# One layer of a hyena and attention backbone: the mixing part's weight remainders and sums moved from GpSimd to VectorE

## The chip, the cores and the metric

The kernel runs on one core of a Trainium2 chip, in float32. The metric is the device time of one execution in microseconds (us), as the median of several runs. TensorE does the matrix products (PE in the profile, PEld its weight loads), VectorE (DVE) and ScalarE (ACT) the elementwise work, GpSimd (POOL) a small share of it, and SyncE (SP) issues the weight transfers.

## The reference

The reference is one layer over 256 latent tokens and 256 context tokens of width 2048. Cut to what matters:

```python
x   = half_ffn(x, ...)                # SwiGLU FFN of width 5632, for latent and context tokens
ctx = half_ffn(ctx, ...)
h, hc = modulate(rms_norm(x)), modulate(rms_norm(ctx))
q, k, v, hy = split_proj(h @ w_in)    # queries, keys, values, and three hyena inputs x0, x1, v
kc, vc = kv_heads(hc @ w_in[:, Q_END:V_END])
attn = block_attention(rope(q), [kc ; rope(k)], [vc ; v])
x0, x1, v = short_conv(hy)            # width 3, centred
v = v * x1
hyo = (long_conv(v) + hy_bias * v) * x0      # convolution through a real FFT of length 512
x = x + gate * (concat(rms_norm(attn), rms_norm(hyo)) @ w_out)
return half_ffn(x, ...)               # second FFN, latent tokens alone
```

## The kernel before, in words

Everything is kept transposed, channels on the 128 partitions and tokens in the free dimension. The full 256 latent and 256 context tokens stand side by side in one 512-column product in the first FFN; the rest of the layer is for latent tokens, with the context only in keys and values.

**A float32 product in pieces.** A float32 operand is cut into a rounded part (`hi`, type fp32r) and a remainder (`lo`), and a product is two or three fp32r products. So each weight tile that arrives (`raw`, 128x1024) needs a cast on ScalarE (`whi`, L192) and a subtraction (`wlo`, L194), before TensorE can use it. The function `weight` does this; its argument `eng` says which engine subtracts, VectorE where none is given:

```python
        S.copy(hi, raw)
        ...
            (eng or V).tensor_sub(lo, raw, hi.bitcast(F32))
```

Activations are cut in the same way (`split` with L176 and L177, `split_to` with L181 and L182; L253 and L254 for the normed inputs). `whi` and `wlo` have three buffers each, `raw` has four.

**The stages of the mixing part, by the time of the profile.** Up to 1533 us the first FFN, of which the last part of the down projection is done twice, first for the context (until 1533) and then for the latent tokens (until about 1556), with the residual sum at L622. While the latent part runs, a hook makes the context's norm: squares on ScalarE (L234), their sums over the eight channel pairs at L241, a product with ones (L245) that adds over partitions, and L215 to L220 for the inverse root. After it come the scaled inputs, one L251, L253 and L254 for each of 16 channel tiles. The projection to keys and values (L653 to L655, `pa`) is done for the context first and then for the latent tokens, with eight weight tiles each, `kp` 0 to 7; the latent norm's steps are put between the context's products by a list in the code, `KV_PLAN`. Then follow the hyena projection (until about 1705), the long convolution (until about 1757; per half and frequency block four products L788 to L791, a difference L796 and a sum L797, and two splits, before the inverse products), and the attention (until about 1850).

**The filler.** The gate `x0` is projected in four column pairs `cp` of four weight tiles `kq` each (`proj_pair`, L208 to L211, 16 matmuls a weight tile, 64 a column pair). It is a generator, of which the attention takes a step where TensorE would wait, and what is left comes at the end of the attention. A column pair's two products lie in two `pa` buffers (there are four for all uses), which come free when L731, the first step of the short convolution (L730 to L734, then L819 multiplies the gate in), has read them. After the attention its group norm (`group_out`: L234, L241, L245, L215 to L220, and then 8 L883 with splits at L181 and L182) gives the first inputs of the output projection `w_o`; the hyena group's norm comes next to its first tiles. The residual's norm (L241, L245) and the second FFN close the layer, from about 1990 on.

**What sets the order.** The code's order is a start only: the framework's scheduler reorders the instructions of each engine by its own costs, and each engine then works off its row in order. So a change of engine moves other instructions as well. The weight transfers are in one queue on SyncE, in the same order before and after.

**The lines on GpSimd before.** `wlo` of every second tile of the last down projection (both parts) and of every second tile of the key and value projection; all 16 `wlo` of the gate; the additions L241 of all norms after the first; L796 and L797; and the `wlo` of every second tile of the second FFN's down projection.

Of the kernel before, what the change touches and what calls it, by code (L numbers as in the profile page):

```python
# [18 lines left out]
P = 128  # L19
# [5 lines left out]
GRP = 4  # L25
# [22 lines left out]
def hybrid_layer_kernel(ctx: ExitStack, tc: tile.TileContext, a):  # L48
    nc = tc.nc
    V, S, G, PE = nc.vector, nc.scalar, nc.gpsimd, nc.tensor  # L50
# [134 lines left out]
    def weight(src, shape, eng=None, behind=None):  # L185
        raw = T(wp, shape, "raw", bufs=4)
        load = nc.sync.dma_start(raw, src)
        if done[0]:
            last_load[0] = load
        hi = T(wp, shape, "whi", F32R, 3)  # L190
        lo = T(wp, shape, "wlo", F32R, 3)
        S.copy(hi, raw)  # L192
        if behind is None:
            (eng or V).tensor_sub(lo, raw, hi.bitcast(F32))  # L194
        else:
            with tc.issue_after(behind.ins):
                V.tensor_sub(lo, raw, hi.bitcast(F32))
        return hi, lo
# [27 lines left out]
    def rstd_steps(pairs, n, y):  # L226

        ps = PB((P, L))
        todo_, acc = [], None
        for q, t in enumerate(pairs):  # L230
            last = q == len(pairs) - 1
            sq = (tmp if last or acc is not None else tmp2)((P, 2, L))
            for part in ((0, 1) if last else (slice(0, 2),)):
                S.activation(sq[:, part, :], t[:, part, :], AF.Square)  # L234
            if last:
                todo_.append(sq)
            elif acc is None:
                acc = sq
                todo_.append(acc)
            else:  # L240
                G.tensor_add(acc, acc, sq)  # L241
        yield
        for q, t in enumerate(todo_):
            for j in range(2):
                PE.matmul(ps, ones, t[:, j, :], start=q == 0 and j == 0, stop=q == len(todo_) - 1 and j == 1)  # L245
        rstd_from(ps, n, (P, L), tmp2, y)
# [22 lines left out]
    class Ffn:  # L269
# [44 lines left out]
        def down(self, g, parts=None, last=None):  # L314

            whole = parts is None
            for dq in range(KT // 2):
                self.hook()
                whi, wlo = weight(self.wdown[g, dq], (P, GRP, 2, P), G if dq % 2 and (not whole or self.np == 1) else None)
                for i2 in range(2):  # L320
                    d = dq * 2 + i2
                    ps = PB((P, 2, L) if whole else (P, L))
                    for jj in range(GRP):
                        act = self.acts[g * GRP + jj]
                        if not whole:
                            act = [t[:, parts, :] for t in act]
                        self.mm(ps, (whi[:, jj, i2, :], wlo[:, jj, i2, :]), act, jj == 0, jj == GRP - 1)
                    if self.np == 1:
                        for half in range(2):
                            V.scalar_tensor_tensor(xd(0, d), ps[:, half, :], mod[0][8][:, d : d + 1], xd(0, d),  # L330
                                                   op0=ALU.mult, op1=ALU.add)
                        if last:
                            last(d)
                        continue
                    for i in range(2) if whole else (parts,):
                        src = ps[:, i, :] if whole else ps
                        if last:
                            last(i, d, src)
                        elif self.gated:
                            V.scalar_tensor_tensor(xd(i, d), src, mod[i][self.cm + 2][:, d : d + 1], xd(i, d),  # L340
                                                   op0=ALU.mult, op1=ALU.add)
                        elif g == 0:
                            S.copy(xd(i, d), src)
                        else:
                            V.tensor_add(xd(i, d), src, xd(i, d))
# [142 lines left out]
    for i in range(2):  # L488
        for q, t in enumerate(xs[i]):
            sq = U((P, 2, L))  # L490
# [18 lines left out]
    for i in range(2):  # L509
        ps = PB((P, L))  # L510
# [32 lines left out]
    with tc.issue_after(copied.ins):  # L543
        w = {j: weight(f1.wup[j, 0], (P, 4, 2, P), behind=lo_last) for j in range(WAVE)}
# [90 lines left out]

    def proj_cols(w, ttiles, share=False, hook=lambda: None):
        ps = []
        for _ in proj_steps(w, ttiles, ps, share):  # L640
            hook()
        return ps

    def proj_steps(w, ttiles, ps, share=False):
        ps += [PA() for _ in ttiles]
        for kp in range(8):
            yield
            whi, wlo = weight(w[kp], (P, 2, 512), G if share and kp % 2 else None)
            for k2 in range(2):
                k = kp * 2 + k2  # L650
                for p_, t in zip(ps, ttiles):
                    hh, hl = ((lat, cont)[t // 2][k][:, s, (t % 2) * P : (t % 2 + 1) * P] for s in range(2))
                    PE.matmul(p_, hh, whi[:, k2, :], start=k == 0, stop=False)  # L653
                    PE.matmul(p_, hh, wlo[:, k2, :], start=False, stop=False)  # L654
                    PE.matmul(p_, hl, whi[:, k2, :], start=False, stop=k == KT - 1)  # L655
# [43 lines left out]
    krot = []  # L699
    also = mix_input(0, lat)  # L700
    plan = iter(KV_PLAN)
    pkv = proj_cols(a["w_kv"], [2, 3], True, lambda: [next((more, also)[s], None) for s in next(plan)])
    for _ in also:
        pass
    pkv += proj_cols(a["w_kv"], [0, 1], True)
    for i in range(4):
        n_ = head_norm(pkv[i], 2)
        if i < 2:
# [26 lines left out]
                               op0=ALU.mult, op1=ALU.add)  # L735
        return y

    def proj_pair(w, out, share=False):
        pa, pb = PA((P, 2, L)), PA((P, 2, L))
        out += [pa, pb]  # L740
        for kq in range(4):
            whi, wlo = weight(w[kq], (P, 4, 2, P), G if share else None)
            for k4 in range(4):
                k = kq * 4 + k4
                for half, ps in ((0, pa), (1, pb)):
                    mm2(ps, (whi[:, k4, half, :], wlo[:, k4, half, :]), lat[k], k == 0, k == KT - 1)
            if kq < 3:
                yield
# [21 lines left out]
    for half in range(2):  # L770
        hs = slice(half * 512, half * 512 + 512)
        vt = []
        for t in range(2):
            pt = PB((P, 4, P))
            for i in range(4):
                ct = half * 4 + i
                PE.transpose(pt[:, i, :], vT[ct // 2][:, ct % 2, t * P : (t + 1) * P], ident)
            vt.append(split(pt.rearrange("p a b -> p (a b)"), (P, 512)))
        yre, yim = [], []
        for f in range(2):  # L780
            pr_, pi_ = PB(), PB()
            for ps, mat in ((pr_, fwd[0]), (pi_, fwd[1])):
                for t in range(2):
                    mm3(ps, [m[:, t, f * P : (f + 1) * P] for m in mat], vt[t], t == 0, t == 1)
            kr, ki = kspec[f][:, hs], kspec[2 + f][:, hs]
            a1, a2 = U((P, 512)), U((P, 512))
            b1, b2 = U((P, 512)), U((P, 512))
            V.tensor_mul(a1, pr_, kr)  # L788
            V.tensor_mul(a2, pi_, ki)
            V.tensor_mul(b1, pr_, ki)  # L790
            V.tensor_mul(b2, pi_, kr)  # L791
            if f == 0:
                V.tensor_copy(b2[0:1, :], a2[0:1, :])
                V.memset(a2[0:1, :], 0.0)
                V.memset(b1[0:1, :], 0.0)
            G.tensor_sub(a1, a1, a2)  # L796
            G.tensor_add(b1, b1, b2)  # L797
            yre.append(split(a1, (P, 512)))
            yim.append(split(b1, (P, 512)))
            for _ in range(QSTEP[2 * half + f]):  # L800
                next(query, None)
        for i in range(4):
            ct = half * 4 + i
            ps = PB((P, L))
            sl = slice(i * P, (i + 1) * P)
            for n, (y_, mat) in enumerate(((yre, inv[0]), (yim, inv[1]))):
                for f in range(2):
                    mm3(ps, [m[:, sl] for m in y_[f]], [m[:, f, :] for m in mat], n + f == 0, n + f == 2)
            V.scalar_tensor_tensor(hyT[ct // 2][:, ct % 2, :], vT[ct // 2][:, ct % 2, :], hyb[:, ct : ct + 1], ps,
                                   op0=ALU.mult, op1=ALU.add)  # L810


    def gate_steps():
        for cp in range(CT // 2):
            p0 = []
            yield from proj_pair(a["w_x0"][cp], p0, True)
            for i in range(2):
                y_ = conv(p0[i], 2 * cp + i)
                V.tensor_mul(hyT[cp][:, i, :], hyT[cp][:, i, :], y_)  # L819
            yield  # L820
# [235 lines left out]
```

## Time and profile before

| What | Value |
|---|---|
| Median of 3 runs | 2743.27 us (2742.76 to 2743.49) |
| Profiled execution | 2740.93 us |
| Its span | 2739.1 us, TensorE clock 0.993 on average |
| TensorE busy | 2680.5 us, 98% |
| VectorE busy | 1866.1 us, 68% |
| GpSimd busy | 235.5 us, 9%, in 113 instructions |
| GpSimd busy from 1480 to 1990 us | 127 us: 32 L194, 22 L241, 4 L796, 4 L797 |
| GpSimd busy after 1990 us | 107.8 us: 44 L194 |

The profiled execution is 2.34 us below the median, and 1.83 us of it lie outside its span. A busy TensorE means only that products follow each other; when it has been idle, the profile's clock column shows whether they run at the full clock. An instruction's duration includes time in which it is held by something that isn't a semaphore, so that the same shape can show two durations; a mean over a line hides this.

### The profile page before, as it was taken

The page shows a single profiled execution, that of the slowest core. Times are in us where ns is not written, and L with a number is a line of the kernel's source. Part 1 is how long each engine was busy: PE and PEld are TensorE (multiplying, and loading weights), DVE is VectorE, ACT ScalarE, POOL GpSimd, SP SyncE. Part 2 cuts the span into 40 slices and gives each one's busy share as a digit, 9 for nine tenths or more (in the row PEclk, how much of TensorE's full clock was granted, in tenths as well). Part 3 has the DMA queues.
Part 4 walks back from the last instruction along what each step waited for, and adds up shares of the span by engine and source line. Part 5 has one row for each costly group of instructions (what it writes and reads, how often), then busy time and mean ns, then how long its engine had stood idle before and what let it go on. Part 6 is the DMA issues. An engine that isn't in the chain of part 4 may idle for free. (4 is left out here: it accounts for less than half of the span.)

```text
span 2739.1 us, 35313 instructions
## 1 busy us (share of the span) xinstructions
PE 2680.5 (98%) x13552; PEld 2232.1 (81%) x13552; DVE 1866.1 (68%) x3044; ACT 962.5 (35%) x1307; POOL 235.5 (9%) x113
## 2 busy tenths in 40 slices
PE   8999999999999999999999999988999999999999
PEld 5678888888888888888888878777788888888888
DVE  6589899976686666434342897878666666666666
ACT  4343222222222222222222555355454444444443
POOL 0000000000000000000000620232111111111111
PEclk9999999999999999999999999999999999999999
DMA  9776666666686666432332455224555555555555
GB/s 381 286 267 213 228 215 219 210 225 210 233 296 224 211 219 216 150 100 96 97 100 93 145 179 185 94 92 140 169 169 185 185 185 186 185 186 187 186 186 170
DMA packets 144352, 513.49 MB, mean 187 GB/s; under 512 B 17175, under 2 KB 21432, under 8 KB 139832
## 3 DMA queue, kind: packets, MB, share of 16 engines
q1 hardware_dynamic: 142456, 508.50, 55.2%
q10 hardware_dynamic: 1728, 2.74, 0.3%
q8 instruction: 107, 1.75, 0.3%
q14 instruction: 61, 0.50, 0.1%
HBM read 506.98 MB, written 4.19 MB: 187 GB/s over the span
## 5 line engine op out<-in xcount | busy, mean ns | idle before, releaser
L192 ACT CAST whi<-raw 128x1024 fp32r<-128x1024 f32 x648 | 680.6, 1051 | 1301.6 <-PE pa L202 489.3
L194 DVE TENSOR_TENSOR wlo<-raw,whi 128x1024 fp32r<-128x1024 f32 x569 | 700.9, 1233 | 490.8 <-ACT whi L192 482.9
L209 PE MATMUL pa<-u,whi 128*128 128x512 f32 x2016 | 715.0, 401 | 10.5 <-DVE u L254 5.9
L201 PE MATMUL pa<-u,whi 128*128 128x512 f32 x1376 | 537.1, 391 | 2.7 <-ACT u L529 2.7
L203 PE MATMUL pa<-u,wlo 128*128 128x512 f32 x1376 | 535.7, 390 | 1.7 <-DVE wlo L194 1.7
L202 PE MATMUL pa<-u,whi 128*128 128x512 f32 x1376 | 536.6, 390 | 0.7 <-DVE u L531 0.7
L211 PE MATMUL pa<-u,wlo 128*128 128x256 f32 x1890 | 533.2, 282 | 2.9 <-POOL wlo L194 1.9
L209 PEld LDWEIGHTS pa<-u,whi 128*128 128x128 f32 x2016 | 377.8, 189 | 98.3 <-issue 6.3
L194 POOL TENSOR_TENSOR wlo<-raw,whi 128x1024 fp32r<-128x1024 f32 x76 | 189.7, 2496 | 2276.3 <-ACT whi L192 2266.0
L211 PEld LDWEIGHTS pa<-u,wlo 128*128 128x128 f32 x1890 | 359.6, 190 | 7.5 <-POOL wlo L194 2.3
L201 PEld LDWEIGHTS pa<-u,whi 128*128 128x128 f32 x1376 | 258.2, 188 | 60.2 <-ACT u L529 4.0
L203 PEld LDWEIGHTS pa<-u,wlo 128*128 128x128 f32 x1376 | 258.1, 188 | 57.6 <-DVE wlo L194 3.1
L202 PEld LDWEIGHTS pa<-u,whi 128*128 128x128 f32 x1376 | 258.6, 188 | 55.3 <-DVE u L531 1.6
L201 PE MATMUL pb<-u,whi 128*128 128x512 f32 (+1 forms) x800 | 299.8, 375 | 2.4 <-DVE u L622 2.4
L203 PE MATMUL pb<-u,wlo 128*128 128x512 f32 (+1 forms) x800 | 298.8, 374 | 2.5 <-DVE wlo L194 2.5
L202 PE MATMUL pb<-u,whi 128*128 128x512 f32 (+1 forms) x800 | 298.7, 374 | 0.0
L209 PE MATMUL pb<-u,whi 128*128 128x512 f32 x736 | 250.3, 399 | 2.2 <-DVE u L330 2.2
L130 DVE CUSTOM_DVE_ANT_0 adas<-adaw,crow,bada 128x1024 bf16<-128x1024 f32 x160 | 205.0, 1281 | 22.1 <-DMA adaw<-in_w_adaT_dram 20.0
L130 DVE CUSTOM_DVE_ANT_0 adas<-adaw,crow,mod 128x1024 bf16<-128x1024 f32 x160 | 205.1, 1282 | 9.8 <-DMA adaw<-in_w_adaT_dram 6.9
L201 PEld LDWEIGHTS pb<-u,whi 128*128 128x128 f32 x800 | 152.0, 190 | 33.7 <-issue 5.0
L203 PEld LDWEIGHTS pb<-u,wlo 128*128 128x128 f32 x800 | 152.1, 190 | 29.0 <-DVE wlo L194 2.7
L202 PEld LDWEIGHTS pb<-u,whi 128*128 128x128 f32 x800 | 151.9, 190 | 26.0
(202 smaller groups left out, 2314.6 us busy)
## 6 DMA issues: line engine op xcount, KB each, us to landing
raw<-in_w_up_dram SPq DMA_DIRECT2D x352, 512.0 KB, 3.6
adaw<-in_w_adaT_dram SPq DMA_DIRECT2D x223, 512.0 KB, 4.9
raw<-in_w_dn_dram SPq DMA_DIRECT2D x184, 512.0 KB, 3.5
wrow<-in_w_ada_dram SPq DMA_DIRECT2D x32, 1024.0 KB, 7.9
raw<-in_w_hy_dram SPq DMA_DIRECT2D x32, 512.0 KB, 3.6
raw<-in_w_o_dram SPq DMA_DIRECT2D x32, 512.0 KB, 3.5
raw<-in_w_kv_dram SPq DMA_DIRECT2D x16, 512.0 KB, 4.1
raw<-in_w_q_dram SPq DMA_DIRECT2D x16, 512.0 KB, 3.5
```

The source lines that it names most:

```text
L130: V.tensor_tensor_reduce(out=sc, in0=t, in1=crow[i][:, b * (D // 2) : (b + 1) * (D // 2)], scale=1.0, scalar=mcol if b else bada[:, n : n ...
L192: S.copy(hi, raw)
L194: (eng or V).tensor_sub(lo, raw, hi.bitcast(F32))
L201: PE.matmul(ps, w[0], xx[0], start=start, stop=False)
L202: PE.matmul(ps, w[0], xx[1], start=False, stop=False)
L203: return PE.matmul(ps, w[1], xx[0], start=False, stop=stop)
L209: PE.matmul(ps, w[0], x, start=start, stop=stop)
L211: PE.matmul(ps[:, 0, :], w[1], x[:, 0, :], start=False, stop=False)
```

## The change

GpSimd keeps only the 44 `wlo` of the second FFN. The 32 other `wlo` subtractions, the 22 additions of squares (L241) and the eight sums of the long convolution (L796, L797) go to VectorE. The same operations are done on the same tiles; 62 instructions change engine.

```diff
@@ rstd_steps
-                G.tensor_add(acc, acc, sq)
+                V.tensor_add(acc, acc, sq)
@@ Ffn.down
-                whi, wlo = weight(self.wdown[g, dq], (P, GRP, 2, P), G if dq % 2 and (not whole or self.np == 1) else None)
+                whi, wlo = weight(self.wdown[g, dq], (P, GRP, 2, P), G if dq % 2 and self.np == 1 else None)
@@ proj_steps (keys and values)
-            whi, wlo = weight(w[kp], (P, 2, 512), G if share and kp % 2 else None)
+            whi, wlo = weight(w[kp], (P, 2, 512))
@@ proj_pair (the gate x0)
-            whi, wlo = weight(w[kq], (P, 4, 2, P), G if share else None)
+            whi, wlo = weight(w[kq], (P, 4, 2, P))
@@ long convolution
-            G.tensor_sub(a1, a1, a2)
-            G.tensor_add(b1, b1, b2)
+            V.tensor_sub(a1, a1, a2)
+            V.tensor_add(b1, b1, b2)
```

The argument `share` falls away with it. The scheduler answers by reordering, and three places matter.

**VectorE, latent keys and values.** Before, `wlo_11928` (`kp` 1) and `wlo_11964` (`kp` 3) are in GpSimd's row, and VectorE's row near `wlo_11946` (`kp` 2) reads:

```order
L251 SCALAR_TENSOR_TENSOR mt_11876<-u_127,mod_4_17_100,u_10982 128x256
L251 SCALAR_TENSOR_TENSOR mt_11881<-u_127,mod_4_17_100,u_10982 128x256
L194 TENSOR_TENSOR wlo_11946<-raw_11943,whi_11945 128x1024
L254 SCALAR_TENSOR_TENSOR u_11870<-mt_11871,mod_3_15_98,u_11870 128x256
L254 SCALAR_TENSOR_TENSOR u_11875<-mt_11876,mod_3_15_98,u_11875 128x256
```

After, VectorE's row there reads:

```order
L251 SCALAR_TENSOR_TENSOR mt_11896<-u_131,mod_4_17_100,u_10982 128x256
L254 SCALAR_TENSOR_TENSOR u_11885<-mt_11886,mod_3_15_98,u_11885 128x256
L254 SCALAR_TENSOR_TENSOR u_11890<-mt_11891,mod_3_15_98,u_11890 128x256
L254 SCALAR_TENSOR_TENSOR u_11895<-mt_11896,mod_3_15_98,u_11895 128x256
L251 SCALAR_TENSOR_TENSOR mt_11901<-u_131,mod_4_17_100,u_10982 128x256
L194 TENSOR_TENSOR wlo_11928<-raw_11925,whi_11927 128x1024
L254 SCALAR_TENSOR_TENSOR u_11900<-mt_11901,mod_3_15_98,u_11900 128x256
L194 TENSOR_TENSOR wlo_11946<-raw_11943,whi_11945 128x1024
L194 TENSOR_TENSOR wlo_11964<-raw_11961,whi_11963 128x1024
```

The remainder of `kp` 1 now stands behind 16 L251 and L254 that follow the remainder of `kp` 0 (`wlo_11910`), and those of `kp` 2 and 3 behind it.

**VectorE, the rotary step of the second query block.** `u_13969` is what TensorE transposes at L870 into `pb_13980`. Before, VectorE's row reads:

```order
L217 RECIPROCAL small_13990<-small_13990 128x4
L688 TENSOR_TENSOR sg_13970<-u_13962,tab_13964 128x256
L689 TENSOR_TENSOR sg_13971<-u_13962,tab_13964 128x256
L692 TENSOR_TENSOR sg_13975<-u_13962,tab_13964 128x256
L690 TENSOR_TENSOR u_13969<-sg_13970,sg_13971 128x256
L218 TENSOR_TENSOR small_13993<-small_13990 128x4
L693 TENSOR_TENSOR sg_13976<-u_13962,tab_13964 128x256
L219 SCALAR_TENSOR_TENSOR small_13993<-small_13993,small_13992 128x4
L694 TENSOR_TENSOR u_13969<-sg_13975,sg_13976 128x256
```

After:

```order
L217 RECIPROCAL small_13990<-small_13990 128x4
L194 TENSOR_TENSOR wlo_14301<-raw_14298,whi_14300 128x1024
L688 TENSOR_TENSOR sg_13970<-u_13962,tab_13964 128x256
L689 TENSOR_TENSOR sg_13971<-u_13962,tab_13964 128x256
L692 TENSOR_TENSOR sg_13975<-u_13962,tab_13964 128x256
L690 TENSOR_TENSOR u_13969<-sg_13970,sg_13971 128x256
L218 TENSOR_TENSOR small_13993<-small_13990 128x4
L194 TENSOR_TENSOR wlo_14371<-raw_14368,whi_14370 128x1024
L693 TENSOR_TENSOR sg_13976<-u_13962,tab_13964 128x256
L219 SCALAR_TENSOR_TENSOR small_13993<-small_13993,small_13992 128x4
L694 TENSOR_TENSOR u_13969<-sg_13975,sg_13976 128x256
```

Two of the gate's remainders are now inside the chain (a third, `wlo_14261`, a few rows ahead of it), and TensorE has 12 more of the gate's products ahead of L870.

**TensorE, the end of the attention.** `pb_14208` is the attention's last product, `pb_14224` the sums of its group norm, and `pa_14450`, `pa_14451` the gate's third column pair, `pa_14556` its fourth. Before:

```order
L203 MATMUL pb_14208<-u_14204,u_12158 128x512
L211 MATMUL pa_14451<-u_11781,wlo_14455 128x256
L209 MATMUL pa_14450<-u_11786,whi_14454 128x512
L211 MATMUL pa_14450<-u_11786,wlo_14455 128x256
L209 MATMUL pa_14451<-u_11786,whi_14454 128x512
L211 MATMUL pa_14451<-u_11786,wlo_14455 128x256
L209 MATMUL pa_14450<-u_11809,whi_14476 128x512
L211 MATMUL pa_14450<-u_11809,wlo_14477 128x256
L209 MATMUL pa_14451<-u_11809,whi_14476 128x512
L211 MATMUL pa_14451<-u_11809,wlo_14477 128x256
L209 MATMUL pa_14450<-u_11814,whi_14476 128x512
L211 MATMUL pa_14450<-u_11814,wlo_14477 128x256
```

After:

```order
L203 MATMUL pb_14208<-u_14204,u_12158 128x512
L245 MATMUL pb_14224<-sg_14225,ones_72 128x256 x2
L245 MATMUL pb_14224<-sq_14233,ones_72 128x256 x2
L209 MATMUL pa_14556<-u_11720,whi_14560 128x512
L211 MATMUL pa_14556<-u_11720,wlo_14561 128x256
```

Before, 53 products of the third column pair stand between `pb_14208` and `pa_14556`, 11 of them ahead of L245. After, the third pair is all done ahead of `pb_14208`, and only the fourth is left behind it.

More of the change, by code (lines that the diff above doesn't have):

```diff
@@ L634, in hybrid_layer_kernel, with proj_cols, proj_steps @@
     f1.down(JT // GRP - 1, 0, residual)
-    def proj_cols(w, ttiles, share=False, hook=lambda: None):
+    def proj_cols(w, ttiles, hook=lambda: None):
         ps = []
-        for _ in proj_steps(w, ttiles, ps, share):
+        for _ in proj_steps(w, ttiles, ps):
             hook()
         return ps
-    def proj_steps(w, ttiles, ps, share=False):
+    def proj_steps(w, ttiles, ps):
         ps += [PA() for _ in ttiles]
@@ L701, in hybrid_layer_kernel @@
     plan = iter(KV_PLAN)
-    pkv = proj_cols(a["w_kv"], [2, 3], True, lambda: [next((more, also)[s], None) for s in next(plan)])
+    pkv = proj_cols(a["w_kv"], [2, 3], lambda: [next((more, also)[s], None) for s in next(plan)])
     for _ in also:
         pass
-    pkv += proj_cols(a["w_kv"], [0, 1], True)
+    pkv += proj_cols(a["w_kv"], [0, 1])
     for i in range(4):
@@ L736, in conv, with proj_pair @@
         return y
-    def proj_pair(w, out, share=False):
+    def proj_pair(w, out):
         pa, pb = PA((P, 2, L)), PA((P, 2, L))
@@ L815, in gate_steps @@
             p0 = []
-            yield from proj_pair(a["w_x0"][cp], p0, True)
+            yield from proj_pair(a["w_x0"][cp], p0)
             for i in range(2):
```

## The prediction

> **What bounds the kernel now.** I read the page's totals, then a table of windows by stage, then what TensorE waits for, and last the timeline at its longest waits.
>
> ```profile
> PE 2680.5 (98%) x13552; PEld 2232.1 (81%) x13552; DVE 1866.1 (68%) x3044; ACT 962.5 (35%) x1307; POOL 235.5 (9%) x113
> ```
>
> TensorE bounds the whole; time can be won or lost only where it stands still or runs at a lower clock. The windows (columns: length, busy PE, PEld, DVE, ACT, POOL, granted clock, DMA share and rate) show where:
>
> ```profile
> 1535.00:1613.00 78.00, 68.42 (x338) 58.17 (x337) 74.24 (x117) 42.35 (x70) 37.71 (x16) 0.91 0.42 141
> 1705.00:1757.00 52.00, 47.88 (x251) 39.49 (x250) 40.86 (x63) 18.44 (x28) 14.39 (x9) 1.00 0.29 92
> 1757.00:1850.00 93.00, 84.23 (x431) 69.19 (x431) 69.49 (x158) 51.07 (x94) 27.06 (x12) 0.96 0.30 96
> 1850.00:1905.00 55.00, 47.68 (x248) 39.92 (x249) 48.26 (x76) 29.89 (x51) 14.75 (x7) 0.94 0.38 125
> 1905.00:1990.00 85.00, 78.48 (x431) 67.55 (x430) 57.81 (x89) 38.23 (x49) 8.64 (x6) 0.96 0.52 167
> 1990.00:2739.00 749.00, 742.32 (x4191) 641.76 (x4189) 501.75 (x753) 330.36 (x441) 107.76 (x44) 1.00 0.57 184
> ```
>
> Five stages of the mixing part hold 36 us in which TensorE is idle (363 less 326.7 busy) and all the lost clock. The second FFN, with its 44 remainders left where they are, is full. From 1535 to 1613, VectorE is busy for 74.2 of 78 us, so work added there looks fatal. What TensorE waits for, from 1531 to 1990 (total, times, longest):
>
> ```profile
> PE pb L870 <- DVE small L220: 4.9, 1, 4.9
> PE pa L654 <- DVE wlo L194: 4.7, 2, 3.2
> PE pb L203 <- DVE wlo L194: 2.5, 1, 2.5
> PE pa L209 <- DVE sg L731: 2.4, 1, 2.4
> PE pb L201 <- DVE u L622: 2.4, 1, 2.4
> PE pa L211 <- POOL wlo L194: 1.9, 1, 1.9
> PE pb L203 <- DVE u L177: 1.9, 4, 0.8
> PE pb L850 <- DVE small L838: 1.5, 1, 1.5
> PE pb L850 <- DVE u L843: 1.3, 1, 1.3
> ```
>
> Nearly all are waits for VectorE. Is its busy time work? The timelines of both engines at two of these waits (start, duration):
>
> ```profile
> 1588.87 1.26 DVE L254 SCALAR_TENSOR_TENSOR u<-mt,mod,u 128x256 fp32r<-128x256 f32 x3
> 1566.20 3.40 POOL L194 TENSOR_TENSOR wlo<-raw,whi 128x1024 fp32r<-128x1024 f32 x1 [3.04 <-ACT whi L192]
> 1567.28 2.61 DVE L254 SCALAR_TENSOR_TENSOR u<-mt,mod,u 128x256 fp32r<-128x256 f32 x1
> 1549.80 2.55 POOL L194 TENSOR_TENSOR wlo<-raw,whi 128x1024 fp32r<-128x1024 f32 x1
> 1550.45 2.98 DVE L194 TENSOR_TENSOR wlo<-raw,whi 128x1024 fp32r<-128x1024 f32 x1
> ```
>
> Three L254 take 1.26 us, 0.42 each; the same one beside a GpSimd subtraction takes 2.61 and ends just after it. A VectorE L194 takes 2.98 and ends 1.1 us after GpSimd's. So VectorE's ops with two SBUF operands stand still while GpSimd runs. [...]
>
> **The change, part by part.** Prices: groups from 1480 to 1990 (count, busy, mean ns):
>
> ```profile
> L194 POOL TENSOR_TENSOR wlo<-raw,whi 128x1024 fp32r<-128x1024 f32 x32 | 82.0, 2561 | 1619.2 <-ACT whi L192 1609.0 <-DVE u L254 3.8 <-DVE small L215 2.8
> L241 POOL TENSOR_TENSOR sg<-sg,sq 128x512 f32<-128x512 f32 x22 | 33.2, 1510 | 92.6 <-ACT sq L234 82.0 <-ACT sg L234 4.2 <-DVE u L622 3.4
> L788 DVE TENSOR_TENSOR u<-pb,kspec 128x512 f32<-128x512 f32 x4 | 2.7, 684 | 1.1 <-PE pb L203 1.1
> L177 DVE TENSOR_TENSOR u<-u,u 128x512 fp32r<-128x512 f32 x8 | 8.1, 1020 | 6.4 <-ACT u L176 6.4
> ```
>
> GpSimd's 62 operations leave with some 127 us (82.0 + 33.2, and 12 for the eight convolution sums at L241's 1.5). VectorE takes 32 L194 at 1.22 (by its mean at the plain hyena projection, the row in the next fence) and 30 additions of 128x512 at 0.68 (L788), 59.4 us. The second term is what VectorE no longer waits. [...]
>
> *Last down projection, keys and values (1535 to 1613).* Groups of VectorE in that window, and the plain L194 from 1613 to 1705, where GpSimd is idle:
>
> ```profile
> L254 DVE SCALAR_TENSOR_TENSOR u<-mt,mod,u 128x256 fp32r<-128x256 f32 x32 | 27.7, 899 | 0.6 <-ACT u L253 0.6
> L251 DVE SCALAR_TENSOR_TENSOR mt<-u,mod,u 128x256 f32<-128x256 f32 x32 | 17.9, 595 | 0.0
> L194 DVE TENSOR_TENSOR wlo<-raw,whi 128x1024 fp32r<-128x1024 f32 x11 | 15.1, 1377 | 0.0
> L194 DVE TENSOR_TENSOR wlo<-raw,whi 128x1024 fp32r<-128x1024 f32 x33 | 40.3, 1222 | 19.0 <-ACT whi L192 18.9
> ```
>
> Held time: 32 x (0.90 - 0.42) + 32 x (0.60 - 0.42) + 11 x (1.38 - 1.22) = 22.9 us. Added here: 10 L194 and 6 L241, 10 x 1.22 + 6 x 0.68 = 16.3 us. VectorE then needs 74.2 - 22.9 + 16.3 = 67.6 of 78 us: fits, with little room. At stake are the waits at L654, L203 and L622 (9.6 us) and the clock: 0.91 over 78 us is 7.0 us. But the new order takes much of it back. With `wlo_11928` behind 16 rows of 0.42, 6.7 us, and its own 1.2, TensorE, having 12 products of 0.23 (2.7 us) per weight tile, waits about 5 us there, where 3.2 was the longest before; the adds L241 also crowd around the first context weights. Laying the rows out by plain durations I get an end 1 to 4 us earlier. Term: -2.5. Ends: -9.6 (all waits gone), and +12.5 as a rival below.
>
> *Long convolution.* Each L796 or L797 pair (GpSimd 3.0 us) becomes 1.4 us on VectorE, in order, ahead of splits (L177) that were held (1.02 against the 0.68 of L788, the same shape). Idle time is 4.1 us. Since ScalarE's part of the split stays in the chain, I take 2.5 of it. Term: -2.5 (0 to -4.1).
>
> *Attention.* The largest wait, L870, is behind a chain with two holds:
>
> ```profile
> 1803.39 2.39 POOL L194 TENSOR_TENSOR wlo<-raw,whi 128x1024 fp32r<-128x1024 f32 x1 [0.57 <-ACT whi L192]
> 1803.47 2.34 DVE L215 TENSOR_SCALAR small<-small 128x4 f32<-128x4 f32 x1
> 1807.06 2.60 POOL L194 TENSOR_TENSOR wlo<-raw,whi 128x1024 fp32r<-128x1024 f32 x1 [1.28 <-ACT whi L192]
> 1807.38 2.56 DVE L692 TENSOR_TENSOR sg<-u,tab 128x256 f32<-128x256 f32 x1
> ```
>
> L215 loses 2.2 and L692 2.1 us (the other rotary steps take 0.42): 4.3 gone, against three remainders in the chain now, 3.7. TensorE has 12 more products ahead, 2.1 us at a mean of 0.175 (0.23 and 0.12 in turn). So the 4.9 us shrink by 0.6 and 2.1, and by more where a remainder fills a wait of the chain for ScalarE; I take 3.5. The two waits at L850 (2.8) lose holds but share VectorE with four new remainders: half, 1.4. The clock, 0.96 over 93 us, cost 3.7 us, partly inside the wait; 2.1 come back. Term: -7.0 (0 to -11.4: 4.9, 2.8 and 3.7).
>
> *End of the attention.* Here the change takes cover away: the gate's third pair is used up earlier. Before, the stretch ran as in these rows:
>
> ```profile
> 1846.87 0.39 PE L203 MATMUL pb<-u,u 128*128 128x512 f32 x1
> 1847.10 0.28 PE L211 MATMUL pa<-u,wlo 128*128 128x256 f32 x1
> 1848.55 1.27 POOL L241 TENSOR_TENSOR sg<-sg,sq 128x512 f32<-128x512 f32 x1 [3.39 <-ACT sq L234]
> 1849.88 1.13 PE L245 MATMUL pb<-sg,ones 128*128 128x256 f32 x4 [0.74 <-POOL sg L241]
> 1854.96 0.43 DVE L731 TENSOR_TENSOR sg<-pa,sg 128x256 f32<-128x256 f32 x1
> 1884.27 1.03 PE L245 MATMUL pb<-sg,ones 128*128 128x256 f32 x4
> ```
>
> From the end T = 1847.10 of `pb_14208` to the hyena group's L245 it took 37.2 us, of which the 149 products between are worth 26.1 (0.175 each): 11.1 lost. After: the sum is there at T+2.1 (1.45, then 0.68 in place of 1.27), and L731, which frees the buffer for `pa_14556`, ends 5.5 later as before (1849.88 to 1855.39): T+7.6, with TensorE idle for 6 us of it, in pieces of 2.1 and some 3.9 about L245. It has 24 products (4.2 us), then needs L731 of `pa_14297`, 21 rows further on VectorE, at 0.4 each 8.4: T+16.0, a wait of 4.2. Then 40 products, 7.0, to the output projection at T+23.0; its ideal is 11.5 (64 products and L245): 11.5 lost, 0.4 more than now. Halved clock comes on top: the 2.5 us wait at L203 brought
>
> ```profile
> 1550.00:1557.00 7.00, 4.54 (x25) 4.17 (x24) 5.98 (x10) 2.59 (x4) 3.63 (x2) 0.76 0.42 143
> ```
>
> a mean clock of 0.76 for 7 us, so 3.4 us at half, costing 1.7 at most. The products after the second wait have it; I add 1.6. [...] Term: +2.0 (-3 to +6).
>
> *Hyena group's norm and the residual's.* The eight L241 fall where VectorE has room (57.8 of 85 us); GpSimd's last holds go. Term: -0.5 (0 to -1.5).
>
> Sum: -2.5 - 2.5 - 7.0 + 2.0 - 0.5 = -10.5. Against the profiled execution, 2740.93, that is 2730.4; the median stands 2.34 above it: 2732.8 us.
>
> **The rivals.** [...]
>
> *Slower:* at keys and values the long durations of VectorE are not GpSimd's doing, but, say, waits within VectorE. Then nothing is recovered there, demand is 74.2 + 16.3 = 90.5 of 78 us, and VectorE is the bound: 12.5 us more, with no gain elsewhere, since the same cause held there: 2755.8 us. It decides as soon as less than some 7 of the 22.9 us come back. Against it: held instructions end with GpSimd's each time, and in the hyena projection, without GpSimd, L194 has its 1222 ns.
>
> *More gained:* all waits named in the terms vanish and the end of the attention gains: -20 or more, below 2723 us.
>
> **How the numbers follow.** About 0.2%, 5.5 us, is what a measurement of this kernel can tell from no change. Chances: forecast 0.58, with a range of its own from 2723 to 2737.8; more gained 0.06; nothing gained 0.20; slower 0.16. So faster 0.64, same 0.20, slower 0.16. The range from 2721 to 2750 leaves out about 0.03 below and 0.12 above.
>
> **What the profile after would show.** VectorE's L254 and L251 near 0.42 from 1535 to 1613, and VectorE busy less than 72 us there; L215 and L692 without their 2.3 and 2.6 us. L870 waiting under 2.5 us. A new wait of 5 to 7 us, in two pieces with L245 between them, at the first L209 after the attention's last product, and one of 3 to 5 behind L731. From 1990 on, nothing changed. The prediction is wrong if TensorE's idle time at keys and values grows by more than 5 us, if the end of the attention loses 17 us or more, or if plain durations don't return.

## The result and the profile after

The changed kernel takes 2728.39 us (median of 6 runs, 2726.85 to 2729.88) against 2742.91 us in the same runs of the kernel before: a ratio of 0.9949, with a 95% interval from 0.9939 to 0.996, so 14.5 us less. The profiled execution's span is 2725.7 us, 13.4 less. The windows of the profile after (busy PE, PEld, DVE, ACT, POOL, granted clock, DMA share and rate):

```profile
1535.00:1613.00 78.00, 67.16 (x343) 56.59 (x342) 68.77 (x133) 43.17 (x70) 0.00 (x0) 0.93 0.42 141
1705.00:1757.00 52.00, 51.94 (x285) 44.64 (x284) 46.21 (x84) 20.05 (x30) 0.00 (x0) 1.00 0.33 104
1757.00:1850.00 93.00, 86.75 (x451) 70.28 (x449) 74.34 (x165) 55.20 (x98) 0.00 (x0) 1.00 0.35 114
1850.00:1905.00 55.00, 50.93 (x278) 43.92 (x279) 50.71 (x96) 31.74 (x52) 0.00 (x0) 0.97 0.43 143
```

VectorE has taken over 16 of GpSimd's operations in the first window and is busy for 5.5 us less. What TensorE waits for, from 1525 to 1990:

```profile
PE pa L654 <- DVE wlo L194: 9.8, 5, 4.4
PE pa L209 <- DVE u L254: 5.9, 1, 5.9
PE pa L209 <- DVE sg L731: 5.7, 2, 3.5
PE pb L245 <- DVE sg L241: 2.1, 1, 2.1
PE pa L209 <- ACT whi L192: 1.0, 1, 1.0
```

L870, L850 and L622 have left the list and L177 is down from 1.9 to 1.2 us; L654 and L731 have grown, and L245 now waits for VectorE. The 5.9 us behind L254 stand in both kernels: it is the first product of the second FFN (at 1981.75 before), which waits for the residual's norm. The prediction's list leaves this longest wait out and calls the one at L870 the largest; since the change doesn't touch it, its sum is none the worse.

Windows of equal times no longer hold equal work, since everything shifts. So the next table has, for each stage, TensorE's loss: the start-to-start times of its products, less 0.227, 0.118 and 0.109 us for products of 512, 256 and 128 columns (the medians of the trace), summed between two marks that are the same in all kernels. It counts waits and a lowered clock together, and short gaps that a busy column hides. The marks are the context norm's L245 and the first transposes of the hyena for the first column, then the convolution's first product (L777), the first L870, the attention's last product, the hyena group's L245, the residual's L245 and the last product. The hyena projection, between the first column and the second, loses 2.0 to 2.6 us in every kernel and is left out. Each line is one profiled execution. A ghost is an operation put on GpSimd only to keep it busy, whose result nobody reads.

| TensorE's loss, us | last down, keys and values | convolution | attention | its end | output projection | second FFN |
|---|---|---|---|---|---|---|
| before | 18.8 | 7.1 | 12.9 | 10.6 | 5.1 | 32.4 |
| after | 18.4 | 1.2 | 4.9 | 11.1 | 3.7 | 33.0 |
| gate on GpSimd | 19.3 | 2.1 | 15.6 | 10.7 | 3.5 | 32.8 |
| sums on GpSimd | 17.9 | 6.0 | 2.9 | 12.3 | 5.0 | 32.3 |
| last down, keys and values on GpSimd | 18.4 | 1.2 | 5.0 | 12.8 | 3.7 | 32.8 |
| ghost subtractions, weight read | 32.3 | 1.2 | 21.5 | 14.1 | 3.8 | 32.0 |
| ghost subtractions, own tile | 32.3 | 1.2 | 18.0 | 14.1 | 3.8 | 32.0 |
| ghost memsets | 18.5 | 1.2 | 6.6 | 12.5 | 3.8 | 33.0 |
| all on VectorE | 20.8 | 1.2 | 5.0 | 12.9 | 3.7 | 25.8 |
| two weights early | 15.8 | 1.2 | 4.6 | 11.6 | 3.7 | 32.4 |
| three early, all on VectorE | 12.2 | 1.2 | 4.6 | 12.9 | 3.7 | 26.5 |

The lines below the second are the experiments.

### The profile page after: what moved, and what is told of

Read it like the earlier page. It is cut to its first block, busy times and chain, and to the rows that moved or that the text cites. A ratio compares the mean times of both kernels' runs of the same rounds, so it can differ in the third digit from the quotient of the medians.

```text
span 2725.7 us, 35248 instructions
## 1 busy us (share of the span) xinstructions
PE 2677.7 (98%) x13552; PEld 2231.1 (82%) x13552; DVE 1870.3 (69%) x3106; ACT 963.0 (35%) x1307; POOL 108.7 (4%) x51
## 4 chain that ended last, share of the span: by engine, by line
PE 94%; DVE 5%; DMA 1%; ACT 1%; issue 0%; ACTq 0%; SPq 0%; DVEq 0%
PE pa L209 17%; PE pa L203 11%; PE pa L201 11%; PE pa L202 11%; PE pa L211 8%; PE pb L201 7%; PE pb L203 7%; PE pb L202 6%; PE pb L209 6%; PE pb L211 2%; DVE u L182 1%; PE pa L654 1%; PE pa L655 1%; PE pb L157 1%; PE pa L653 1%; PE pb L208 1%
## 5 line engine op out<-in xcount | busy, mean ns | idle before, releaser
L194 DVE TENSOR_TENSOR wlo<-raw,whi 128x1024 fp32r<-128x1024 f32 x601 | 734.5, 1223 | 507.4 <-ACT whi L192 495.7
L130 DVE CUSTOM_DVE_ANT_0 adas<-adaw,crow,bada 128x1024 bf16<-128x1024 f32 x160 | 205.1, 1282 | 17.9 <-DMA adaw<-in_w_adaT_dram 15.8
L194 POOL TENSOR_TENSOR wlo<-raw,whi 128x1024 fp32r<-128x1024 f32 x44 | 107.7, 2448 | 2607.7 <-ACT whi L192 2607.7
```

The source lines that it names most:

```text
L130: V.tensor_tensor_reduce(out=sc, in0=t, in1=crow[i][:, b * (D // 2) : (b + 1) * (D // 2)], scale=1.0, scalar=mcol if b else bada[:, n : n ...
```

## Experiments

All are edits of the changed kernel, and each time is a median beside runs of the kernel before on the same chip (2742.8, 2742.9 and 2743.2 us for the three groups of runs).

**One part back on GpSimd.** Three kernels undo one part of the change each.

```diff
-   whi, wlo = weight(self.wdown[g, dq], ..., G if dq % 2 and self.np == 1 else None)
+   whi, wlo = weight(self.wdown[g, dq], ..., G if dq % 2 and (not whole or self.np == 1) else None)
-   whi, wlo = weight(w[kp], (P, 2, 512))
+   whi, wlo = weight(w[kp], (P, 2, 512), G if share and kp % 2 else None)
```

> The changed kernel, but with the 8 remainders of the last down projection and the 8 of the key and value projection that sat on GpSimd back on GpSimd; the gate and all sums stay on VectorE. Theory (VectorE is held while GpSimd reads, and what the change won is the holds that went): L251 and L254 go back to means above 0.55 us; since this stage won nothing by the change (0.6 us lost), the time stays near the changed kernel's: 2726 to 2731 us. Rival (the change of order is what counts, not the holds): the remainder behind 16 rows of L251 and L254 is gone, and with it a wait of 4.6 us, so 2723 to 2725 us.

Measured: 2727.71 us (2726.77 to 2728.44), ratio to before 0.9945 (0.9933 to 0.9958). VectorE's groups from 1535 to 1613 of this kernel:

```profile
L254 DVE SCALAR_TENSOR_TENSOR u<-mt,mod,u 128x256 fp32r<-128x256 f32 x32 | 25.7, 843 | 1.1 <-ACT u L253 1.1
L251 DVE SCALAR_TENSOR_TENSOR mt<-u,mod,u 128x256 f32<-128x256 f32 x32 | 16.0, 538 | 0.0
```

L254 is back at 0.84 us, and the stage's loss is what it was, 18.4 us. On balance it is the same to TensorE in this stage whether VectorE is held or does the work. The rows also stand in another order here, yet a wait of 4.2 us for a remainder is still there, which the rival expected to be gone. (The mean of L251 misses the expected bound by a little.)

```diff
-   whi, wlo = weight(w[kq], (P, 4, 2, P))
+   whi, wlo = weight(w[kq], (P, 4, 2, P), G if share else None)
```

> The changed kernel, but with the 16 remainders of the gate back on GpSimd. Theory (holds): the attention stage gives back most of the 11 us that it won: 2736 to 2740 us, with VectorE ops of 2.3 to 2.6 us there again. Rival (the gain of the attention stage came from the sums L241 and from the order): 2728 to 2731 us.

Measured: 2738.73 us (2737.05 to 2739.84), ratio 0.9984 (0.9975 to 0.9993). This part alone takes back 10.3 of the 14.5 us. TensorE's waits from 1757 to 1850 in this kernel:

```profile
PE pb L870 <- DVE small L220: 4.9, 1, 4.9
PE pb L850 <- DVE small L838: 2.6, 2, 1.4
PE pb L850 <- DVE u L843: 2.2, 2, 1.2
```

The wait at L870 is 4.9 us again, to the digit, though all sums are on VectorE, and the four L692 of this stage have a mean of 953 ns, where each takes 0.42 us in the changed kernel. The order changes too, so this run alone does not part the holds from the order; the runs with ghosts below do.

```diff
-   V.tensor_add(acc, acc, sq)
+   G.tensor_add(acc, acc, sq)
-   V.tensor_sub(a1, a1, a2)
-   V.tensor_add(b1, b1, b2)
+   G.tensor_sub(a1, a1, a2)
+   G.tensor_add(b1, b1, b2)
```

> The changed kernel, but with the 22 sums of squares (L241) and the 8 sums of the long convolution back on GpSimd. Theory (holds, and a shorter chain): the convolution's 2.6 us and the 1.4 us of the output projection are given back: 2731 to 2734 us. Rival (only the weight remainders count): 2727 to 2730 us.

Measured: 2731.33 us (2728.96 to 2731.99), ratio 0.9957 (0.9945 to 0.997). The convolution loses 6.0 instead of 1.2 us, the output projection 5.0 instead of 3.7 and the attention's end 12.3 instead of 11.1; the attention loses 2.0 less, in another order of rows, and no run shows why. So the sums are worth about 3 us on balance (the intervals of the ratios overlap) and 4.8 in the convolution. That is mostly not a hold. The convolution's splits (L177) and sums in this kernel, and its splits in the changed kernel (1705 to 1757):

```profile
L177 DVE TENSOR_TENSOR u<-u,u 128x512 fp32r<-128x512 f32 x8 | 6.2, 790 | 5.7 <-ACT u L176 5.7
L796 POOL TENSOR_TENSOR u<-u,u 128x512 f32<-128x512 f32 x4 | 6.1, 1534 | 9.8 <-issue 4.8 <-DVE u L789 3.3 <-DVE u L794 1.8
```

```profile
L177 DVE TENSOR_TENSOR u<-u,u 128x512 fp32r<-128x512 f32 x8 | 5.3, 683 | 1.1 <-ACT u L176 1.1
```

The holds come to 0.9 us in all (6.2 less 5.3, two of the eight splits), while a sum takes 1.5 us on GpSimd and 0.66 on VectorE, and TensorE waits behind the sums and their splits (four times for L177, 1.9 us from 1705 to 1757; in the changed kernel no wait is listed there).

**Holds alone, with nothing else changed.** Undoing a part lets the scheduler reorder, so these runs mix holds and order. The next three leave every row of the other engines in the changed kernel's order and only give GpSimd something to do at the old places.

```diff
+   if ghost:                       # the 32 remainders that the change moved
+       G.tensor_sub(gh, hi.bitcast(F32), hi.bitcast(F32))
```

> The changed kernel, with every instruction of TensorE, VectorE, ScalarE and SyncE in the same order, and 32 extra subtractions of 128x1024 on GpSimd, one for each remainder that the change moved: each reads the weight's rounded part twice and writes a tile that nobody reads. Theory (holds): VectorE is held again for 2.5 us each time, now on top of the work it has taken over, so the keys and values stage loses some 8 to 16 us and the attention some 8 to 12: 2740 to 2756 us, and L251 and L254 have means above 0.55 us again. Rival (the gain is the new order, and GpSimd's work itself costs VectorE nothing): 2727 to 2731 us, with all means as in the changed kernel.

Measured: 2753.97 us (2753.43 to 2761.48), ratio 1.0047 (1.0033 to 1.0061): 25.6 us above the changed kernel, for work that no product needs. Two of the five runs took 2758.9 and 2761.5 us, the profiled one among them, so this kernel's line of the table holds some 5 us more than its median. The two lines of VectorE from 1535 to 1613 (L254 and L257 are L251 and L254 here):

```profile
L254 DVE SCALAR_TENSOR_TENSOR mt<-u,mod,u 128x256 f32<-128x256 f32 x32 | 18.4, 614 | 0.0
L257 DVE SCALAR_TENSOR_TENSOR u<-mt,mod,u 128x256 fp32r<-128x256 f32 x32 | 17.1, 575 | 0.0
```

The next two take apart what such an operation does: it writes and reads, and it keeps the weight's buffer.

```diff
+       G.tensor_copy(g2[:, 0:4], h2.bitcast(F32))     # sets the moment
+       for _ in range(2):
+           G.memset(g2, 0.0)
```

> The changed kernel with the same order on all other engines, and on GpSimd, for each of the 32 remainders that the change moved, a copy of 128x4 from the weight's rounded part (it sets the moment) and then two memsets of 128x1024 to a tile that nobody reads. Theory (VectorE is held by GpSimd's reads): the memsets read nothing, so 2728 to 2733 us, and L251 and L254 keep means below 0.50 us. Rival (any GpSimd work in SBUF holds VectorE): 2740 us or more, and means above 0.55 us.

Measured: 2730.06 us (2729.22 to 2731.7), ratio 0.9956 (0.9943 to 0.9968). GpSimd's groups from 1480 to 1990 and VectorE's two from 1535 to 1613 (L262 and L265 are L251 and L254 here):

```profile
L208 POOL MEMSET gh<- 128x1024 f32 x64 | 61.2, 957 | 3.8
L206 POOL COPY gh<-whi 128x4 f32<-128x4 f32 x32 | 37.5, 1171 | 658.4 <-ACT whi L194 658.1
L262 DVE SCALAR_TENSOR_TENSOR mt<-u,mod,u 128x256 f32<-128x256 f32 x32 | 13.9, 473 | 0.0
L265 DVE SCALAR_TENSOR_TENSOR u<-mt,mod,u 128x256 fp32r<-128x256 f32 x32 | 13.8, 473 | 0.0
```

GpSimd is busy for 99 us, and these lines keep the means of the changed kernel (482 and 483 ns); the time is 1.7 us above it, with ranges that overlap.

The last one is shown against the kernel with memsets.

```diff
-       for _ in range(2):
-           G.memset(g2, 0.0)
+       G.tensor_sub(g2, g2, g2)
```

> The same as the kernel with memsets, but in place of the two memsets one subtraction of 128x1024 on GpSimd that reads a tile of its own twice and writes it. No weight buffer is held any longer than by the copy of 128x4. Theory (holds): as with the subtractions that read the weight, 2745 to 2757 us. Rival (the ghost subtractions cost time because they kept the weight's buffer and so ScalarE's casts waiting): 2728 to 2734 us.

Measured: 2755.91 us (2755.39 to 2757.43), ratio 1.0049 (1.0035 to 1.0063). The same groups (L261 and L264 are L251 and L254 here):

```profile
L207 POOL TENSOR_TENSOR gh<-gh 128x1024 f32<-128x1024 f32 x32 | 68.1, 2128 | 2.6
L264 DVE SCALAR_TENSOR_TENSOR u<-mt,mod,u 128x256 fp32r<-128x256 f32 x32 | 18.1, 607 | 0.0
L261 DVE SCALAR_TENSOR_TENSOR mt<-u,mod,u 128x256 f32<-128x256 f32 x32 | 17.0, 570 | 0.0
```

So it is not GpSimd's being busy that holds VectorE, and not the weight's buffer: 32 subtractions on a tile that no other engine touches (2128 ns each) cost 25.9 us more than 64 memsets (957 ns each), of about the same length in all. In the table the keys and values lose 13.9 us more than in the changed kernel, and the attention 13.1. The subtraction reads and the memset doesn't (`gh<-gh` and `gh<-` in the rows); they are also different instructions, and a large copy, which reads one tile, was not tried. Which of these differences makes the hold is not shown.

**The rest of GpSimd's work.**

```diff
-   whi, wlo = weight(self.wdown[g, dq], (P, GRP, 2, P), G if dq % 2 and self.np == 1 else None)
+   whi, wlo = weight(self.wdown[g, dq], (P, GRP, 2, P))
```

> The changed kernel with the last 44 remainders, those of the second FFN's down projection, on VectorE too. TensorE is idle for 5.4 of 735 us there, and VectorE has 491 us of work in them, so there is little to win: theory 2725 to 2729 us. Rival (holds cost in this stage as well, though the waits are short): 2722 to 2725 us.

Measured: 2722.47 us (2721.58 to 2725.09), ratio 0.9929 (0.9917 to 0.9942). The expectation's theory is wrong here, and its rival's range holds: a stage that looked full still had 7.2 us (33.0 to 25.8) to give. The groups of L182 after 1990, in the changed kernel and then in this one:

```profile
L182 DVE TENSOR_TENSOR u<-sg,u 128x256 fp32r<-128x256 f32 x43 | 38.1, 886 | 2.1 <-ACT u L181 2.1
```

```profile
L182 DVE TENSOR_TENSOR u<-sg,u 128x256 fp32r<-128x256 f32 x44 | 18.5, 420 | 2.1 <-ACT u L181 2.1
```

and TensorE's waits there, before this edit and after:

```profile
PE pb L209 <- DVE u L330: 2.2, 11, 0.2
```

```profile
PE pb L209 <- DVE u L330: 0.2, 1, 0.2
```

Once in each of the eleven groups a held L182 (2.42 us in place of 0.42) delays L330, which empties the buffer for the next product. In ten of the groups this costs TensorE two stretched products, 0.37 and 0.08 us, 4.5 us in all; the last group's stretch of 0.34 and 0.08 is there after this edit as well. Against that this kernel has 13 new stretches of 0.10 us. About half of the 7.2, 3.5 us, is made of differences of less than 0.02 us at each of some 4200 products, and no run shows their cause.

**The order at keys and values.**

```diff
+   early = {kp: weight(a["w_kv"][kp], (P, 2, 512)) for kp in range(2)}
    for _ in also:
        pass
    ...
-           whi, wlo = weight(w[kp], (P, 2, 512))
+           whi, wlo = early.get(kp) or weight(w[kp], (P, 2, 512))
    ...
-   pkv += proj_cols(a["w_kv"], [0, 1])
+   pkv += proj_cols(a["w_kv"], [0, 1], early=early)
```

> The changed kernel, with the first two weight tiles of the latent keys and values written in the code ahead of the last scaled inputs, so that the remainder of kp 1 stands further ahead in VectorE's row. Theory (what ate the keys and values stage's gain is the remainder behind 16 rows of L251 and L254): the wait of 4.6 us there shrinks by 2 to 4 us, 2724 to 2727 us. Rival (VectorE's throughput binds this part, and the wait only moves to the next weight): 2728 to 2729 us.

Measured: 2723.86 us (2723.25 to 2724.8), ratio 0.9932 (0.992 to 0.9945). TensorE's wait from 1580 to 1613, in the changed kernel and then in this one:

```profile
PE pa L654 <- DVE wlo L194: 6.7, 2, 4.4
```

```profile
PE pa L654 <- DVE wlo L194: 4.7, 2, 2.8
```

The time is a little below the theory's range. The stage loses 15.8 instead of 18.4 us: the row order named in the prediction was a cause there, and can be mended. These 2.6 us are the larger part of the 4.5; the rest is spread over other stages.

**Together.** All three kernels have the 44 remainders of the second FFN on VectorE. The first has two early weights with that; the second has `range(3)` for the early weights; the third has two early weights, and the latent norm's sums one step later in `KV_PLAN`.

> Both steps that helped, together: the first two latent key and value weights written earlier, and all of GpSimd's remainders, the second FFN's too, on VectorE. Theory (they act in different stages and add up: 4.5 and 5.9 us less than the changed kernel's 2728.4): 2717 to 2720 us. Rival (the early weights win by an order that the other edit undoes): 2721 to 2724 us.

Measured: 2718.45 us (2716.37 to 2719.05), ratio 0.9907 (0.9892 to 0.9921). The gains add up: 9.9 us below the changed kernel, of 4.5 and 5.9.

> The same, with the first three latent weights written earlier. Theory (this part is bound by VectorE's throughput once the first weights are ahead, so a third brings nothing): within 2 us of the kernel with two. Rival (each weight that stands further ahead wins as much): 2 to 4 us less than with two.

Measured: 2715.53 us (2714.11 to 2716.92), ratio 0.9898 (0.9881 to 0.9914). TensorE's wait from 1580 to 1613:

```profile
PE pa L654 <- DVE wlo L194: 1.9, 1, 1.9
```

The third weight brings 2.9 us more (the intervals of the ratios overlap, the ranges of the runs only just: 2716.37 to 2719.05 and 2714.11 to 2716.92), and the stage's loss is down to 12.2. This is what the rival expected: VectorE's throughput doesn't bind this part yet. The kernel has the lowest median here.

```diff
-KV_PLAN = ((0, 0, 1), (0, 0), (0, 0), ...
+KV_PLAN = ((0, 0), (0, 0, 1), (0, 0), ...
```

> The same as with two weights, with the latent norm's squares and their six sums one weight tile later among the context's keys and values. Theory (the sums crowd the first context weights, where TensorE waits 2.5 us): that wait shrinks by 1 to 2 us, 2715 to 2718 us. Rival (the norm then ends later and the latent part waits for it): 1 to 4 us more than with two weights.

Measured: 2717.14 us (2715.61 to 2718.09), ratio 0.9903 (0.9888 to 0.9917). No difference from the kernel with two early weights can be told (2718.45, with ranges that overlap). Inconclusive.

## Why the prediction was right

The forecast was 2732.8 us, with the holds on VectorE as its mechanism; the kernel takes 2728.4, inside the forecast's own range. Term by term, in the table's losses:

- *Holds.* L254 and L251 from 1535 to 1613 went from 899 and 595 ns to

```profile
L251 DVE SCALAR_TENSOR_TENSOR mt<-u,mod,u 128x256 f32<-128x256 f32 x32 | 14.1, 482 | 0.0
L254 DVE SCALAR_TENSOR_TENSOR u<-mt,mod,u 128x256 fp32r<-128x256 f32 x32 | 14.0, 483 | 0.0
```

  and VectorE's busy time to 68.8 us, where the arithmetic gave 67.6. The rival in which the long durations have another cause is refuted by this and by the ghost kernels.
- *Keys and values*, term -2.5, measured -0.4. The wait of "about 5 us" behind the 16 rows is the one of 4.4; but the stage's waits as laid out were enough to eat all of the gain, and the term was still put at a gain. The end came 0.6 us later (first transposes of the hyena, 1613.89 and 1614.52), not 1 to 4 earlier.
- *Convolution*, term -2.5 with an end of -4.1, measured -5.9. This was the worst-sized term, and it lies outside its own bounds. The end was read from TensorE's busy column, 4.1 us idle, and the loss by start-to-start times is 7.1. A product of 512 columns is shown as 0.39 us long though the next one can start after 0.227, so the column hides the first 0.16 us of each delay, and 9 products were delayed by more than 0.15. The chain's saving was also cut for ScalarE without a row. And the splits were not held throughout: of the eight that make the mean of 1.02 us, three were (1.11, 1.10 and 2.52), and five took 0.68. As the kernel with the sums on GpSimd shows, most of this gain is the shorter sum.
- *Attention*, term -7.0, measured -8.0. The chain's two holds are gone, and the remainders stand in it, as these rows of the timeline after show:

```profile
1799.05 1.19 DVE L194 TENSOR_TENSOR wlo<-raw,whi 128x1024 fp32r<-128x1024 f32 x1
1800.83 0.42 DVE L692 TENSOR_TENSOR sg<-u,tab 128x256 f32<-128x256 f32 x1
1801.58 1.22 DVE L194 TENSOR_TENSOR wlo<-raw,whi 128x1024 fp32r<-128x1024 f32 x1
1803.17 0.43 DVE L694 TENSOR_TENSOR u<-sg,sg 128x256 f32<-128x256 f32 x1
```

  L870 starts at 1803.65, right behind the end of L694 at 1803.60, with no wait listed: the products ahead of it fill the time. The granted clock is 1.00 from 1757 to 1850.
- *End of the attention*, term +2.0, measured +0.5. The new waits stand where they were foretold, in these rows (the second one is the product after the first wait):

```profile
1842.87 0.40 PE L203 MATMUL pb<-u,u 128*128 128x512 f32 x1
1845.35 1.10 PE L245 MATMUL pb<-sg,ones 128*128 128x256 f32 x4 [2.08 <-DVE sg L241]
1850.86 0.80 PE L209 MATMUL pa<-u,whi 128*128 128x512 f32 x1 [3.55 <-DVE sg L731]
1859.05 0.47 PE L209 MATMUL pa<-u,whi 128*128 128x512 f32 x1 [2.17 <-DVE sg L731]
```

  2.1 and 3.6 us against 2.1 and 3.9; the last is 2.2 instead of 4.2, and of the 3 to 5 that were to be seen in the profile. Its end was right: the product starts 15.95 us after T, the end of the first row's product at 1843.10, where T+16.0 was forecast. But the 24 products before it take 5.9 us instead of 4.2, since the first ten run at some 0.64 us a pair instead of 0.35 (granted clock 0.76 from 1850 to 1857, and 0.50 from 1851 to 1854; the kernel before has 0.50 from 1554 to 1556, behind the wait that the term's half was taken from). The term added 1.6 us for that on top of the wait; it fell inside the wait, because L731 ends it and not TensorE. Without the 1.6 the term is +0.4, close to the +0.5 measured, although the clock did fall to 0.50.
- *Output projection*, term -0.5, measured -1.4. *Second FFN*, no term, measured +0.6, close to the nothing that was foretold.

The stages' sum is -14.6 against -10.5; the first mark comes 1.0 us later than before and the hyena projection loses 0.2 more, so the span shrinks by 13.4. The direction rested on one reading, that a GpSimd operation beside a VectorE one makes its duration two to six times as long (2.98 us for 1.22, 2.61 for 0.42). That reading held for subtractions and sums: the plain durations came back, and the ghost subtractions took them away again (means of 482 and 483 ns, then 614 and 575). It was too wide for "while GpSimd runs", since the memsets left them at 473. Time came back with the plain durations in the attention, but not at keys and values, and in the convolution most of the gain is not a hold. What the working got wrong were sizes, in the convolution above all; that the 2.1 us too much forecast at keys and values stand against the 3.4 too little in the convolution, so that the total came out nearer than these terms, is luck.

## What to carry to other kernels

Before giving GpSimd a share of elementwise work, look at VectorE's durations beside it: where the same shape shows two durations, and the long ones end with GpSimd's (before, an L215 of 2.34 us ending at 1805.81, an L194 of GpSimd at 1805.78), the share can cost more than it saves, even in stages whose engines look full or free (2722.5 us with none of it on GpSimd, 2742.9 with all of it). It need not: at keys and values the holds and the work came out even (18.4 us lost either way). The 64 memsets, 61.2 us of GpSimd's time, cost nothing here that can be told from the spread (2730.06 us, 2729.22 to 2731.7, against 2728.39, 2726.85 to 2729.88). When work is moved to another engine, look next at what the scheduler put in its row ahead of the first instruction that TensorE needs (here 16 rows of L251 and L254, and a wait of 4.4 us); writing that instruction earlier in the code was worth 4.5 us here, and 2.9 more for one more weight.

## What was not expected

In two places a GpSimd operation was the long one, beside VectorE operations of plain duration. In the kernel with the ghosts that read the weight (start, duration; L257 is L254 there):

```profile
1591.10 6.00 POOL L200 TENSOR_TENSOR gh<-whi 128x1024 f32<-128x1024 f32 x1 [5.10 <-ACT whi L192]
1594.13 1.22 DVE L194 TENSOR_TENSOR wlo<-raw,whi 128x1024 fp32r<-128x1024 f32 x1
1595.27 2.91 DVE L257 SCALAR_TENSOR_TENSOR u<-mt,mod,u 128x256 fp32r<-128x256 f32 x3
```

An operation of 2.6 us on average took 6.00: VectorE ran its rows at plain durations until about 1595.3 (L194 in 1.22), and then its three L257 took 2.91 in place of 1.27. In the kernel with its own tile, a copy of only 128x4 took 4.32 us on GpSimd at 1594.62, where one at 1587.73 took 1.30; VectorE ran at plain durations until 1598.8, and then two L264 took 2.51. That GpSimd waited for VectorE in the first part is a reading of these rows; what ended it just then is not shown.

The prediction spoke of VectorE's operations with two operands in SBUF. Operations with one input there were long beside GpSimd's too: L215 of 128x4 in the prediction's rows (2.34 us; 0.17 after), and in the kernel with the gate on GpSimd two of the 16 L843 of 128x512 (1.88 and 1.83 us; 0.48 for the others; the mean is 652 ns, and 483 in the changed kernel). One L622, which takes one of its inputs from PSUM, was not: in the kernel before it took its 0.47 us at 1550.05, in the middle of a GpSimd subtraction that ran from 1549.80 to 1552.35.
